# A decoder layer with a product-key expert stage on one core: the gate spread is stretched over more expert blocks, and six blocks' activations stay on chip

## The chip, the cores and the metric

One core of one Trainium2 chip runs the whole layer in one launch. The time is that of the device, in microseconds, for one execution; lower is better. The engines of the core are TensorE (PE, with its weight loads as PEld), VectorE (DVE), ScalarE (ACT), GpSimd (POOL) and SyncE (SP, which here only issues DMAs). Sixteen DMA engines serve all queues.

## What is computed

One layer over 1024 tokens of width 1024, all in float32: attention and a convolution group, a first layer norm, then the expert stage ("PEER"), a gated embedding and a second layer norm. The change touches the expert stage and the first load of the last one.

```python
def peer(x, w_query, sub_keys, u_table, v_table):          # tables: 16384 experts x 1024
    q = (xt @ w_query).reshape(t, 8, 2, 128)
    sc = einsum('thpc,hpnc->thpn', q, sub_keys)
    top_s, top_i = top_k(sc, 16)                            # per head and half
    best_s, best_c = top_k(top_s[:, :, 0, :, None] + top_s[:, :, 1, None, :], 16)
    ids = i1 * 128 + i2                                     # 128 experts per token
    gates = softmax(best_s)
    h = einsum('cd,ced->ce', x, u_table[ids])
    act = gelu(h) * gates
    return einsum('ce,ced->cd', act, v_table[ids])
...
r = ALPHA * x + peer(x, ...)
e = sigmoid(r @ w_gate) * (p @ w_ple)
x = LN2(r + e)
```

## The kernel before

The 1024 tokens are 8 tiles of 128. Tiles 0 to 2 (group A) and tiles 3 to 7 (group B, 640 tokens, `ND`) go through the expert stage in two different ways that run at the same time.

**Group A: rows.** `s_gather` fetches, for each of the 128 experts of a token, one row of U and one row of V. One step fetches 128 rows, one for each token of a tile, with an indirect DMA on GpSimd's queue (line 769, 512 KB), and VectorE uses it `ROWLAG` = 3 steps later: a product with `x1` summed into `hb` (line 777), or a multiply-add into `ag` (line 785). There are 3 x 256 = 768 such rows, with `UB` = 7 buffers. `behind` puts a row's use behind the fourth last entry of a list of marks, on VectorE's queue.

**Group B: dense.** All 16384 experts are computed for the 640 tokens, in 128 blocks of 128 experts:

- *U* (`s_early`, `u_half`): a block of U is loaded (512 KB), turned by 8 TensorE transposes, split into a high and a low part (`uu`), and multiplied with x in three products (lines 158 to 160, `mm3`), 48 matmuls of 320 columns. The low part is made by VectorE (line 665), or by TensorE with one more matmul of 512 columns for each half block and a ScalarE copy (lines 672, 674, `by_pe`). Then ScalarE takes the gelu (line 699), and the block's activations go to memory in `e_dr` (320 KB, line 700).
- *Choice* (`s_choose`): VectorE finds the experts and gates of each token of group B.
- *Spread* (`s_gates`): the gates of a token are spread over all 16384 experts as a product of two one-hot matrices. For four tokens at a time VectorE makes two comparisons (line 740) and two products (line 743) of 512 bf16 elements a partition, ScalarE makes four more products (line 745), TensorE 12 matmuls of 128 columns (line 750), ScalarE copies the sums into `stage` (line 752). Each 32 tokens the stage (2 MB) is stored in `g_dr` (line 754). A run has 160 such steps.
- *V* (`s_dense`): in sets of `SET` = 3 blocks, `v_block` loads a block of V (512 KB) and splits it (`vh`, `vl`), loads the activations from `e_dr`, multiplies them by the gates (line 878, from `gt`, six blocks a load), and splits them (`ah`, `al`), all in rings of `RING` = 7. `products` then multiplies: for each of 10 outputs, 9 matmuls of 512 columns a set. Seven outputs have a PSUM bank for the whole run (`sum`); three share one bank (`part`) and are added to `acc` by VectorE after each set (line 899).

**Order.** A program-order interleave, `weave`, puts the streams together; on it a scheduler orders each engine's queue at build time, and the queue then runs in that order. After the front part (`ORDER`) the stages are: queries of group B beside `UQ` = 9 U blocks and `RQ` = 105 rows; the choice beside `UC` = 14 blocks and `RC` = 5 rows; the spread beside 40 blocks and `RG` = 160 rows; the remaining blocks beside `RU` = 180 rows; the V stage beside the other 318 rows. The gathering pool, `VA` (U and V loads, activation buffers, `GEB` = 3) and `GT` (gates) lie on the left of SBUF; x of group B and the pages, and later the V pool, on the right.

**Final stage.** `turned` transposes and splits `r`, `gated` multiplies with the gate and embedding weights, loaded in four chunks of 256 columns by `weights` (lines 932 to 936). Its pool `Z` lies where the gathering pool was.

Of the kernel before, what the change touches and what calls it, by code (L numbers as in the profile page):

```python
# [19 lines left out]
P = 128  # L20
# [32 lines left out]
RQ, RC, RG, RU = 105, 5, 160, 180  # L53
TIE = 4
RX = 2
ZC = 3
# [20 lines left out]
def run(gen):  # L77
    for _ in gen:
        pass
# [17 lines left out]
def layer(tc, io):  # L97
# [578 lines left out]
    def s_early():  # L676

        aH, aL = act[1]
        halves = [(c, h) for c in range(P) for h in range(2)]
        ready = []  # L680
        for n in range(AHEAD):
            ready.append(u_half(*halves[n]))
            u_rest()
        for n, (c, h) in enumerate(halves):
            u_rest()
            if n + AHEAD < len(halves):
                ready.append(u_half(*halves[n + AHEAD]))
            uu = ready.pop(0)
            if h == 0:
                pss = [ph()[:, :cn] for _, cn in spl]  # L690
            for k in range(4):
                kk = 4 * h + k
                for o, (c0, cn) in zip(pss, spl):
                    mm3(o, uu[:, 0, k, :], uu[:, 1, k, :], aH[:, kk, c0:c0 + cn], aL[:, kk, c0:c0 + cn],
                              kk == 0, kk == KD - 1)
            if h:
                ge = page([P, ND], F32, "ge") if c < UA + UQ + UC else VA.tile([P, ND], F32, name="ge", bufs=GEB)
                for o, (c0, cn) in zip(pss, spl):
                    nc.scalar.activation(ge[:, c0:c0 + cn], o, AF.Gelu)
                nc.sync.dma_start(e_dr[c], ge)  # L700
                yield


    def s_gates(S_):

        iota4 = S_.tile([P, 4, P], BF, name="iota4")
        nc.vector.tensor_copy(iota4, iota_b[:, None, :].to_broadcast([P, 4, P]))

        def pairs(a):
            return a.rearrange("p e (n d) -> p e n d", d=2)  # L710
# [1 line left out]
        for j, i in enumerate(GB):  # L712
# [16 lines left out]
            nc.vector.tensor_tensor(rest, rest, sT[:, 3, :, 0], op=OP.subtract)  # L729
            for tb in range(P // TB):  # L730
                stage = S_.tile([P, P, TB], F32, name="stage", bufs=2)
                for q in range(TB // 4):
                    t = tb * TB + 4 * q

                    def col(k):
                        return sT[:, k, t:t + 4, None, :].to_broadcast([P, 4, P // 2, 2])

                    oo = S_.tile([P, 2, 4, P], BF, name="oo", bufs=2)
                    for k in range(2):
                        nc.vector.tensor_tensor(pairs(oo[:, k]), pairs(iota4), col(k), op=OP.is_equal)  # L740
                    o2 = S_.tile([P, 3, 4, P], BF, name="o2", bufs=OB)
# [6 lines left out]
                    for e in range(4):  # L748
# [4 lines left out]
                    if q == TB // 4 - 1:  # L753
# [80 lines left out]
    close(WP_p)  # L834
    VA_p, VA = pool("dense_a", "left")
    S_p, S_ = pool("spread", "left")
    weave((s_gates(S_), ND // 4), (early, SPILL - UF - UA - UQ - UC), (rows, RG))
    close(S_p)


# [5 lines left out]

    def gates(c):

        m = min(GG * SET, P - c)
        gts[c] = GT.tile([P, NB, GG * SET, TB], F32, name="gt", bufs=2)  # L850
        nc.sync.dma_start(gts[c][:, :, :m, :], g_dr[:, :, c * TB:(c + m) * TB].rearrange("b i (a t) -> i b a t", t=TB))

    left = P * 2 * NA - RQ - RC - RG - sum(int(v[2:]) for w in ORDER.split("|") for v in w.split() if v[0] == "r")
    weave((early, P - SPILL + UF), (rows, RU))
    left -= RU
# [10 lines left out]
    A_hi, A_lo, V_hi, V_lo = {}, {}, {}, {}  # L866

    def v_block(c, gt, k):
# [6 lines left out]
        ge = VA.tile([P, ND], F32, name="ge", bufs=GEB)  # L875
        nc.sync.dma_start(ge, e_dr[c])
        v = ge.rearrange("p (b t) -> p b t", t=TB)
        nc.vector.tensor_tensor(v, v, gt[:, :, k, :], op=OP.mult)  # L878
        A_hi[c] = V.tile([P, ND], F32R, name="ah", bufs=RING)
        A_lo[c] = V.tile([P, ND], F32R, name="al", bufs=RING)  # L880
        split(A_hi[c], A_lo[c], ge, nc.vector)

    def prepare(cs):
        if cs[0] % (GG * SET) == 0 and cs[0] + GG * SET < P:
            gates(cs[0] + GG * SET)
        for c in cs:
            v_block(c, gts[c - c % (GG * SET)], c % (GG * SET))
            yield

    def products(cs, o):  # L890

        j, h = o
        i, sl, hs = GB[j], slice(j * P, (j + 1) * P), slice(512 * h, 512 * h + 512)
        ps = sums[o] if o in sums else PO.tile([P, 512], F32, name="part", bufs=1)
        for c in cs:
            mm3(ps, A_hi[c][:, sl], A_lo[c][:, sl], V_hi[c][:, hs], V_lo[c][:, hs],
                c == (0 if o in sums else cs[0]), c == (P - 1 if o in sums else cs[-1]))
        if o not in sums or cs[-1] == P - 1:
            marks.append(nc.vector.tensor_tensor(acc[i][:, hs], acc[i][:, hs], ps, op=OP.add))

    def s_dense():

        sets = [list(range(c, min(c + SET, P))) for c in range(0, P, SET)]
        gates(0)
        run(prepare(sets[0]))
        for n, cs in enumerate(sets):
            ahead = prepare(sets[n + 1]) if n + 1 < len(sets) else iter(())
# [5 lines left out]
            run(ahead)  # L913

    dense = s_dense()
    n = len(outs) * -(-P // SET)
    weave((dense, n - RX), (rows, left))
    weave((dense, RX))
    run(rows)
    run(dense)  # L920
    close(V_p)
# [1 line left out]
    PP_p, PP = banks("psum_last")  # L923


    cn = 256
    wg, rT, r, bs = {}, {}, {}, {}
    ZR_p, ZR = pool("final_r", "right")

    def weights(c, pool_, eng):  # L930
        cs = slice(c * cn, (c + 1) * cn)
        raw = ZR.tile([P, KD + 2, cn], F32, name="wraw", bufs=1)
        nc.sync.dma_start(raw[:, :KD, :], io["ple_gate"][0][:, cs].rearrange("(k p) n -> p k n", p=P))
        nc.sync.dma_start(raw[:, KD:, :], io["ple_proj"][0][:, cs].rearrange("(k p) n -> p k n", p=P))
        wg[c] = [pool_.tile([P, KD + 2, cn], F32R, name=f"w{x}{c}") for x in "hl"]
        split(*wg[c], raw, eng)

    weights(0, ZR, nc.vector)
    lg, lb = bcast(io["ln2_g"][0], "ln2_g", ZR), bcast(io["ln2_b"][0], "ln2_b", ZR)
    close(GT_p)  # L940
    close(VA_p)
    close(G_p)
# [80 lines left out]
```

## Time and profile before

| | |
|---|---|
| time, median of 3 runs (lowest to highest) | 2925.62 us (2921.28 to 2936.11) |
| the profiled execution, its own time | 2930.05 us |
| its span, first to last instruction | 2928.2 us |
| mean granted TensorE clock | 0.975 of 2.4 GHz |
| TensorE, VectorE, ScalarE, GpSimd busy | 95%, 83%, 41%, 37% |
| moved by DMA | 778.11 MB, 266 GB/s over the span |

The profile is one execution. A matmul's duration in it includes a pipelined tail, so that durations of neighbours overlap; the pace is read from how many start in a stretch. A share of the DMA is the mean busy share of the 16 engines. In a row, "<-" after an idle time names what ended the wait.

### The profile page before, as it was taken

Reading aid. Unit: us, or ns where it says so; the run is one execution under the profiler, and the core shown is the slowest. Engines: PE = TensorE matmul, PEld = TensorE weight load, DVE = VectorE, ACT = ScalarE, POOL = GpSimd, SP = SyncE. Lnnn points to the kernel's source line nnn. Section 1 sums busy time; section 2 is a strip of 40 time slices with the busy share of each in tenths; the row PEclk is TensorE's granted clock in tenths of the full one; section 3 lists DMA queues with packets and bytes.
Section 4 is the critical chain, followed back from the end, with each engine's and each line's share of the span. In section 5 each row is a group of like instructions: output and inputs, shape, how many; then the busy total and the mean of one; then the engine's idle time right before and its main releaser. Section 6 shows DMA issues by size and latency. Waiting matters only on the chain.

```text
span 2928.2 us, 47594 instructions
## 1 busy us (share of the span) xinstructions
PE 2794.5 (95%) x17615; PEld 2513.3 (86%) x17615; DVE 2437.2 (83%) x5461; ACT 1193.6 (41%) x2464; POOL 1078.1 (37%) x851
## 2 busy tenths in 40 slices
PE   8996899999999999999999999799899999999888
PEld 8974589999999999999999999687788787777688
DVE  7999768979989799999856666898899888778866
ACT  4454634433334788888622222222222222222143
POOL 0103010267600333443435555555454445444320
PEclk9996899999999999999999999999999999999999
DMA  5211343599913699999999999999999999989631
GB/s 158 76 51 40 99 127 103 183 369 321 349 60 113 239 352 344 334 346 338 364 352 328 338 337 343 364 357 358 352 356 360 358 371 348 323 309 316 215 125 53
DMA packets 324569, 778.11 MB, mean 266 GB/s; under 512 B 29137, under 2 KB 144337, under 8 KB 321776
## 3 DMA queue, kind: packets, MB, share of 16 engines
q0 software_dynamic: 110592, 402.70, 38.0%
q1 hardware_dynamic: 213744, 372.37, 36.5%
q8 instruction: 138, 2.26, 0.3%
q14 instruction: 95, 0.78, 0.1%
HBM read 683.75 MB, written 91.23 MB: 265 GB/s over the span
## 4 chain that ended last, share of the span: by engine, by line
PE 79%; DVE 11%; DMA 5%; issue 3%; ACT 2%; SPq 0%; POOL 0%; DVEq 0%; ACTq 0%; POOLq 0%
PE ph L158 15%; PE ph L159 14%; PE ph L160 14%; PE sum L159 6%; PE sum L158 5%; PE sum L160 5%; PE pv L750 4%; PE pt L659 3%; PE part L158 2%; PE part L159 2%; PE part L160 2%; DMA ge<-e_dr 2%; DVE ag L785 2%; DVE row L777 1%; DVE vl L150 1%
## 5 line engine op out<-in xcount | busy, mean ns | idle before, releaser
L769 POOL DMA_INDIRECT row<-in_peer_u_dram,ids x384 | 511.5, 1332 | 707.9 <-DVE ag L785 418.7
L769 POOL DMA_INDIRECT row<-in_peer_v_dram,ids x384 | 499.5, 1301 | 647.0 <-DVE row L777 480.0
L158 PE MATMUL ph<-acth,uu 128*128 128x320 f32 x2048 | 657.4, 321 | 0.1
L159 PE MATMUL ph<-actl,uu 128*128 128x320 f32 x2048 | 641.6, 313 | 0.0
L160 PE MATMUL ph<-acth,uu 128*128 128x320 f32 x2048 | 639.9, 313 | 0.0
L785 DVE SCALAR_TENSOR_TENSOR ag<-row,hb,ag 128x1024 f32<-128x1024 f32 x384 | 492.4, 1282 | 2.2 <-DMA row<-in_peer_v_dram,ids 1.3
L777 DVE SCALAR_TENSOR_TENSOR row<-row,x 128x1024 f32<-128x1024 f32 x384 | 467.9, 1222 | 5.5 <-DMA row<-in_peer_u_dram,ids 5.2
L158 PEld LDWEIGHTS ph<-acth,uu 128*128 128x128 f32 x2048 | 386.6, 189 | 1.4 <-ACT sg L558 0.4
L159 PEld LDWEIGHTS ph<-actl,uu 128*128 128x128 f32 x2048 | 386.9, 189 | 0.7
L160 PEld LDWEIGHTS ph<-acth,uu 128*128 128x128 f32 x2048 | 385.5, 189 | 0.4
L159 PE MATMUL sum<-vl,ah 128*128 128x512 f32 x896 | 353.7, 395 | 5.0 <-DVE vl L150 4.8
L158 PE MATMUL sum<-vh,ah 128*128 128x512 f32 x896 | 344.2, 397 | 4.2 <-ACT ah L154 2.8
L154 ACT CAST ah<-ge 128x640 fp32r<-128x640 f32 x128 | 93.3, 729 | 570.7 <-DVE ge L878 417.4
L160 PE MATMUL sum<-vh,al 128*128 128x512 f32 x896 | 267.4, 390 | 0.0
L661 ACT CAST uu<-pt 128x512 fp32r<-128x512 f32 x256 | 150.5, 590 | 190.8 <-PE pt L659 181.0
L745 ACT ACTIVATE o<-oo,rest 128x128 bf16<-128x128 bf16 x640 | 205.8, 399 | 21.4 <-DVE oo L740 16.6
L158 PEld LDWEIGHTS sum<-vh,ah 128*128 128x128 f32 x896 | 171.0, 191 | 45.4 <-ACT ah L154 5.4
L159 PEld LDWEIGHTS sum<-vl,ah 128*128 128x128 f32 x896 | 171.3, 191 | 43.2 <-DVE vl L150 7.1
L158 PE MATMUL part<-vh,ah 128*128 128x512 f32 x384 | 154.7, 403 | 47.2 <-ACT ah L154 30.1
L160 PEld LDWEIGHTS sum<-vh,al 128*128 128x128 f32 x896 | 168.5, 188 | 34.9
L150 DVE TENSOR_TENSOR vl<-raw,vh 128x1024 fp32r<-128x1024 f32 x128 | 154.7, 1220 | 40.8 <-ACT vh L154 40.4
L150 DVE TENSOR_TENSOR uu<-pt,uu 128x512 fp32r<-128x512 f32 x116 | 79.8, 689 | 127.7 <-ACT uu L661 118.9
(298 smaller groups left out, 5768.3 us busy)
## 6 DMA issues: line engine op xcount, KB each, us to landing
raw<-in_peer_v_dram SPq DMA_DIRECT2D x128, 512.0 KB
raw<-in_peer_u_dram SPq DMA_DIRECT2D x89, 512.0 KB
e_dr<-ge SPq DMA_DIRECT2D x128, 320.0 KB
g_dr<-stage SPq DMA_DIRECT2D x20, 2048.0 KB
ge<-e_dr SPq DMA_DIRECT2D x128, 320.0 KB
gt<-g_dr SPq DMA_DIRECT2D x21, 1920.0 KB
uraw<-in_peer_u_dram SPq DMA_DIRECT2D x39, 512.0 KB
wraw<-in_peer_query_dram SPq DMA_DIRECT2D x32, 512.0 KB
```

The source lines that it names most:

```text
L150: return eng.tensor_tensor(o, a, b, op=OP.subtract)
L154: nc.scalar.copy(hi, src)
L158: nc.tensor.matmul(ps, lh, rh, start=first, stop=False)
L159: nc.tensor.matmul(ps, lh, rl, start=False, stop=False)
L160: nc.tensor.matmul(ps, ll, rh, start=False, stop=last)
L659: nc.tensor.matmul(ps[:, k * P:(k + 1) * P], raws[c][:, (4 * h + k) * P:(4 * h + k + 1) * P], ident, is_transpose=True, start=k == 0, stop ...
L661: nc.scalar.copy(uu[:, 0], turned)
L745: nc.scalar.mul(o2[:, 2, e], oo[:, 1, e], rest[:, t + e:t + e + 1])
L750: nc.tensor.matmul(ps[:, e * P:(e + 1) * P], o2[:, m, e], oo[:, 0, e], start=m == 0, stop=m == 2)
L769: nc.gpsimd.indirect_dma_start(out=t, out_offset=None, in_=table, in_offset=bass.IndirectOffsetOnAxis(ap=ids[i][:, s:s + 1], axis=0))
L777: behind(nc.vector.scalar_tensor_tensor(u, u, 1.0, x1, op0=OP.mult, op1=OP.mult, accum_out=hb[:, e:e + 1]), marks, TIE)
L785: behind(nc.vector.scalar_tensor_tensor(ag, v, blocks[b][:, e:e + 1], ag, op0=OP.mult, op1=OP.add), marks, TIE)
```

## The change

- The spread runs beside U until block 118 (`SPILL` 80 to 118) and takes eight tokens an instruction: 80 steps with instructions of 1024 elements and two PSUM tiles each; `o2` has 2 buffers instead of 3. TensorE still makes the low parts only for blocks below 80 (`ULOW`); the point from which one half in four goes to VectorE moves from block 39 to 47, since it hangs on `UC`.
- `UC` 14 to 22, `RC` 5 to 45 (choice), `RG` 160 to 295 (spread, beside 70 blocks), `RU` 180 to 48 (the last 13 blocks). 275 rows remain for the V stage.
- The activations of the last `KEEP` = 6 blocks are gated and split where they are made (`gated_split`), in a pool of their own, and are neither stored nor loaded. The V stage starts with these six. The ring of `ah` and `al` is that pool, six buffers.
- The first chunk of the final weights is loaded into a buffer of `gt`, issued behind the last dense step and ahead of the last rows.

```diff
-SPILL = 80
+SPILL = 118
+ULOW = 80
+KEEP = 6
-PAGES, WPAGES, RAWS, GEB, OB = 5, 6, 3, 3, 3
+PAGES, WPAGES, RAWS, GEB, OB = 5, 6, 3, 3, 2
-UA, UQ, UC, UF = 14, 9, 14, 3
-RQ, RC, RG, RU = 105, 5, 160, 180
+UA, UQ, UC, UF = 14, 9, 22, 3
+RQ, RC, RG, RU = 105, 45, 295, 48
...
-        by_pe = c < SPILL and not (2 * c > edge and c % 2 == h == 0)
+        by_pe = c < ULOW and not (2 * c > edge and c % 2 == h == 0)
...
-                nc.sync.dma_start(e_dr[c], ge)
+                if c < P - KEEP:
+                    nc.sync.dma_start(e_dr[c], ge)
+                else:
+                    gated_split(c, ge)
...
-                for q in range(TB // 4):
-                    t = tb * TB + 4 * q
+                for q in range(TB // 8):
+                    t = tb * TB + 8 * q
...
-                    ps = pv()
-                    for e in range(4):
-                        for m in range(3):
-                            nc.tensor.matmul(ps[:, e * P:(e + 1) * P], o2[:, m, e], oo[:, 0, e],
-                                             start=m == 0, stop=m == 2)
-                    nc.scalar.copy(stage[:, :, 4 * q:4 * q + 4], ps.rearrange("p (t n) -> p n t", t=4))
+                    for f4 in range(2):
+                        ps = pv()
+                        for e in range(4):
+                            for m in range(3):
+                                nc.tensor.matmul(ps[:, e * P:(e + 1) * P], o2[:, m, 4 * f4 + e], oo[:, 0, 4 * f4 + e],
+                                                 start=m == 0, stop=m == 2)
+                        nc.scalar.copy(stage[:, :, 8 * q + 4 * f4:8 * q + 4 * f4 + 4], ps.rearrange("p (t n) -> p n t", t=4))
...
+    AC_p, AC = pool("dense_acts", "left")
+    group = GG * SET
+    starts = [P - KEEP, *range(0, P - KEEP, group)]
+    first, final = P - KEEP, P - KEEP - 1
+
+    def gated_split(c, ge):
+        k = (c - first) if c >= first else c
+        gt = gts[c - k % group]
+        v = ge.rearrange("p (b t) -> p b t", t=TB)
+        nc.vector.tensor_tensor(v, v, gt[:, :, k % group, :], op=OP.mult)
+        A_hi[c] = AC.tile([P, ND], F32R, name="ah", bufs=KEEP)
+        A_lo[c] = AC.tile([P, ND], F32R, name="al", bufs=KEEP)
+        split(A_hi[c], A_lo[c], ge, nc.vector)
+
+    gates(first)
...
+        if c < first:
+            ge = VA.tile([P, ND], F32, name="ge", bufs=GEB)
+            nc.sync.dma_start(ge, e_dr[c])
+            gated_split(c, ge)
...
+    sets = [list(range(c, min(c + SET, n))) for b, n in ((first, P), (0, first)) for c in range(b, n, SET)]
...
+    raw0 = GT.tile([P, NB, group, TB], F32, name="gt", bufs=2).rearrange("p b a t -> p (b a t)")
+    raw0 = raw0[:, :(KD + 2) * cn].rearrange("p (k n) -> p k n", n=cn)
+    last_weights(0, raw0)
     run(rows)
     run(dense)
```

## Rows read from the trace of the kernel before

**Rows 1.** The page, part 1: busy us, share of the span, instructions.

```profile
PE 2794.5 (95%) x17615; PEld 2513.3 (86%) x17615; DVE 2437.2 (83%) x5461; ACT 1193.6 (41%) x2464; POOL 1078.1 (37%) x851
```

**Rows 2.** Windows: length; busy us (count) of PE, PEld, DVE, ACT, POOL; PE clock, DMA share, GB/s.

```profile
1000.00:1400.00 400.00, 400.00 (x3664) 372.45 (x3664) 368.34 (x771) 327.37 (x874) 162.22 (x135) 1.00 0.93 342
...
1500.00:1800.00 300.00, 300.00 (x2123) 299.30 (x2122) 204.85 (x278) 79.46 (x159) 156.71 (x129) 1.00 0.95 333
1840.00:1910.00 70.00, 64.60 (x271) 51.89 (x272) 61.25 (x78) 16.40 (x20) 35.64 (x28) 0.97 0.98 358
1910.00:2270.00 360.00, 349.29 (x1515) 285.28 (x1514) 320.33 (x406) 88.66 (x107) 180.54 (x132) 0.99 0.99 358
2270.00:2550.00 280.00, 268.00 (x1159) 218.24 (x1158) 242.78 (x309) 67.88 (x82) 141.00 (x99) 0.99 0.98 354
2550.00:2600.00 50.00, 50.00 (x220) 41.35 (x219) 39.73 (x51) 11.53 (x14) 20.72 (x14) 0.99 0.85 296
2600.00:2750.00 150.00, 142.26 (x607) 114.01 (x606) 119.11 (x148) 29.64 (x38) 69.36 (x48) 0.99 0.86 301
```

**Rows 3.** Timeline at the turn from U to V: start, us, engine, what.

```profile
1825.52 2.94 ACT L154 CAST vh<-raw 128x1024 fp32r<-128x1024 f32 x3
...
1826.07 0.38 SPq L876 DMA_DIRECT2D ge<-e_dr  x1
...
1838.26 0.82 DVE L878 TENSOR_TENSOR ge<-ge,gt 128x640 f32<-128x640 f32 x1
...
1839.88 0.79 PE L158 MATMUL part<-vh,ah 128*128 128x512 f32 x1 [15.18 <-ACT ah L154]
```

**Rows 4.** Timeline at the start of the final stage.

```profile
2784.20 2.33 ACT L154 CAST wh<-wraw 128x2560 fp32r<-128x2560 f32 x1 [31.73 <-DMA wraw<-in_ple_proj_dram]
...
2789.86 1.07 ACT L154 CAST rTh<-pt 128x512 fp32r<-128x512 f32 x2 [3.34 <-DMA r_dr<-ag]
...
2790.50 0.58 PE L158 MATMUL ph<-wh,rTh 128*128 128x256 f32 x1 [10.57 <-ACT rTh L154]
```

**Rows 5.** Waits, TensorE, 1840 to 2750: us in total, times, longest.

```profile
PE part L158 <- ACT ah L154: 30.1, 8, 15.2
PE part L158 <- DVE acc L899: 11.9, 10, 2.0
```

**Rows 6.** DMA queues, 1840 to 2750: packets, MB, share of 16 engines.

```profile
q0 software_dynamic: 46265, 168.46, 50.6%
q1 hardware_dynamic: 87392, 144.04, 44.7%
```

**Rows 7.** Timeline of VectorE at the end of the choice.

```profile
963.81 0.23 DVE L714 CAST f<-i1b 128x128 f32<-128x128 bf16 x1 [10.16 <-PE pt L718]
```

**Rows 8.** Windows of line 750 alone: PE busy (count), PEld, clock, DMA.

```profile
1000.00:1400.00 400.00, 139.37 (x1620) 98.79 (x1619) 1.00 0.93 342
```

**Rows 9.** DMA queues, 1000 to 1400.

```profile
q0 software_dynamic: 19529, 71.14, 50.1%
q1 hardware_dynamic: 12837, 64.85, 42.8%
```

**Rows 10.** DMA queues, 1500 to 1800.

```profile
q0 software_dynamic: 18263, 66.51, 62.9%
q1 hardware_dynamic: 11201, 33.14, 31.7%
```

**Rows 11.** Lines of VectorE by form, 1000 to 1400: busy us, mean ns, idle before.

```profile
L740 DVE TENSOR_TENSOR oo<-iota,sT 128x512 bf16<-128x512 bf16 x270 | 102.9, 424 | 26.2 <-PE pv L750 19.8 <-ACT o L745 2.3 <-issue 1.9
...
L785 DVE SCALAR_TENSOR_TENSOR ag<-row,hb,ag 128x1024 f32<-128x1024 f32 x77 | 98.5, 1280 | 0.2
L777 DVE SCALAR_TENSOR_TENSOR row<-row,x 128x1024 f32<-128x1024 f32 x58 | 70.7, 1218 | 0.0
L150 DVE TENSOR_TENSOR uu<-pt,uu 128x512 fp32r<-128x512 f32 x18 | 12.3, 685 | 0.8 <-ACT uu L661 0.8
```

**Rows 12.** Lines by form, whole run: a bf16 instruction of 1024 elements.

```profile
L575 DVE TENSOR_TENSOR u<-ge 128x1024 bf16<-128x1024 bf16 x16 | 11.6, 722 | 0.1
```

More of the change, by code (lines that the diff above doesn't have):

```diff
@@ L699, in s_early @@
                     nc.scalar.activation(ge[:, c0:c0 + cn], o, AF.Gelu)
-                nc.sync.dma_start(e_dr[c], ge)
+                if c < P - KEEP:
+                    nc.sync.dma_start(e_dr[c], ge)
+                else:
+                    gated_split(c, ge)
                 yield
     def s_gates(S_):
-        iota4 = S_.tile([P, 4, P], BF, name="iota4")
-        nc.vector.tensor_copy(iota4, iota_b[:, None, :].to_broadcast([P, 4, P]))
+        iota8 = S_.tile([P, 8, P], BF, name="iota8")
+        nc.vector.tensor_copy(iota8, iota_b[:, None, :].to_broadcast([P, 8, P]))
         def pairs(a):
@@ L731, in s_gates @@
                 stage = S_.tile([P, P, TB], F32, name="stage", bufs=2)
-                for q in range(TB // 4):
-                    t = tb * TB + 4 * q
+                for q in range(TB // 8):
+                    t = tb * TB + 8 * q
                     def col(k):
-                        return sT[:, k, t:t + 4, None, :].to_broadcast([P, 4, P // 2, 2])
-                    oo = S_.tile([P, 2, 4, P], BF, name="oo", bufs=2)
+                        return sT[:, k, t:t + 8, None, :].to_broadcast([P, 8, P // 2, 2])
+                    oo = S_.tile([P, 2, 8, P], BF, name="oo", bufs=2)
@@ L739, in s_gates @@
                     for k in range(2):
-                        nc.vector.tensor_tensor(pairs(oo[:, k]), pairs(iota4), col(k), op=OP.is_equal)
-                    o2 = S_.tile([P, 3, 4, P], BF, name="o2", bufs=OB)
+                        nc.vector.tensor_tensor(pairs(oo[:, k]), pairs(iota8), col(k), op=OP.is_equal)
+                    o2 = S_.tile([P, 3, 8, P], BF, name="o2", bufs=OB)
                     for m in range(2):
                         mark = nc.vector.tensor_tensor(pairs(o2[:, m]), pairs(oo[:, 1]), col(2 + m), op=OP.mult)
-                    for e in range(4):
+                    for e in range(8):
@@ L836, in layer @@
     S_p, S_ = pool("spread", "left")
-    weave((s_gates(S_), ND // 4), (early, SPILL - UF - UA - UQ - UC), (rows, RG))
+    weave((s_gates(S_), ND // 8), (early, SPILL - UF - UA - UQ - UC), (rows, RG))
     close(S_p)
@@ L847, in gates @@
     def gates(c):
-        m = min(GG * SET, P - c)
+        m = min(group, (P if c >= first else first) - c)
         gts[c] = GT.tile([P, NB, GG * SET, TB], F32, name="gt", bufs=2)
         nc.sync.dma_start(gts[c][:, :, :m, :], g_dr[:, :, c * TB:(c + m) * TB].rearrange("b i (a t) -> i b a t", t=TB))
+    AC_p, AC = pool("dense_acts", "left")
+    A_hi, A_lo, V_hi, V_lo = {}, {}, {}, {}
+    group = GG * SET
[10 more added lines that the diff above has]
+    gates(first)
     left = P * 2 * NA - RQ - RC - RG - sum(int(v[2:]) for w in ORDER.split("|") for v in w.split() if v[0] == "r")
@@ L874, in v_block @@
         split(V_hi[c], V_lo[c], raw, nc.vector)
[L875 to L881, printed above, removed]
+        if c < first:
+            ge = VA.tile([P, ND], F32, name="ge", bufs=GEB)
+            nc.sync.dma_start(ge, e_dr[c])
+            gated_split(c, ge)
     def prepare(cs):
-        if cs[0] % (GG * SET) == 0 and cs[0] + GG * SET < P:
-            gates(cs[0] + GG * SET)
+        if cs[0] in starts and starts.index(cs[0]) + 1 < len(starts):
+            gates(starts[starts.index(cs[0]) + 1])
         for c in cs:
-            v_block(c, gts[c - c % (GG * SET)], c % (GG * SET))
+            v_block(c)
             yield
@@ L896, in products @@
             mm3(ps, A_hi[c][:, sl], A_lo[c][:, sl], V_hi[c][:, hs], V_lo[c][:, hs],
-                c == (0 if o in sums else cs[0]), c == (P - 1 if o in sums else cs[-1]))
-        if o not in sums or cs[-1] == P - 1:
+                c == (first if o in sums else cs[0]), c == (final if o in sums else cs[-1]))
+        if o not in sums or cs[-1] == final:
             marks.append(nc.vector.tensor_tensor(acc[i][:, hs], acc[i][:, hs], ps, op=OP.add))
+    sets = [list(range(c, min(c + SET, n))) for b, n in ((first, P), (0, first)) for c in range(b, n, SET)]
     def s_dense():
-        sets = [list(range(c, min(c + SET, P))) for c in range(0, P, SET)]
-        gates(0)
         run(prepare(sets[0]))
@@ L915, in layer, with last_weights @@
     dense = s_dense()
-    n = len(outs) * -(-P // SET)
+    n = len(outs) * len(sets)
     weave((dense, n - RX), (rows, left))
+    cn = 256
+    def last_weights(c, raw):
+        cs = slice(c * cn, (c + 1) * cn)
+        nc.sync.dma_start(raw[:, :KD, :], io["ple_gate"][0][:, cs].rearrange("(k p) n -> p k n", p=P))
+        nc.sync.dma_start(raw[:, KD:, :], io["ple_proj"][0][:, cs].rearrange("(k p) n -> p k n", p=P))
     weave((dense, RX))
+    raw0 = GT.tile([P, NB, group, TB], F32, name="gt", bufs=2).rearrange("p b a t -> p (b a t)")
+    raw0 = raw0[:, :(KD + 2) * cn].rearrange("p (k n) -> p k n", n=cn)
+    last_weights(0, raw0)
     run(rows)
@@ L930, in weights @@
     def weights(c, pool_, eng):
[L931 to L934, printed above, removed]
+        if c:
+            raw = ZR.tile([P, KD + 2, cn], F32, name="wraw", bufs=1)
+            last_weights(c, raw)
         wg[c] = [pool_.tile([P, KD + 2, cn], F32R, name=f"w{x}{c}") for x in "hl"]
-        split(*wg[c], raw, eng)
+        split(*wg[c], raw if c else raw0, eng)
     weights(0, ZR, nc.vector)
     lg, lb = bcast(io["ln2_g"][0], "ln2_g", ZR), bcast(io["ln2_b"][0], "ln2_b", ZR)
+    close(AC_p)
     close(GT_p)
```

7 lines of the change are left out of this document (2 added, 5 removed).

## The prediction

> **What bounds the kernel now.** I read the page first: TensorE is busy 95% of the span [rows 1]. So the question is where TensorE is kept from running at its pace, and the windows by stage answer it [rows 2]. In the spread stage (1000 to 1400 us) it is busy all 400 us, and no wait of TensorE is listed there; in the plain U stage (1500 to 1800 us) likewise. There 2123 matmuls start in 300 us, 0.141 us each, so a block of 56 costs 7.91 us. The V stage is different: its counts fall below the 220 that the undisturbed window from 2550 us fits into 50 us (0.227 us each). From 1840 to 2750 us it starts 271 + 1515 + 1159 + 220 + 607 = 3772 matmuls, worth 857 us at that pace, in 910 us: 53 us lost. Ahead of that stands the wait of 15.18 us at the turn from U to V [rows 3], and behind the last sum another of 10.57 us [rows 4]. The change touches all of these, so it can gain; what it loads in return is the spread stage, whose room has to be worked out.
>
> Next I asked why the V stage loses. Its waits name the activation casts and the adds that free the one `part` bank [rows 5]. Behind them stand two nearly full servants. DMA: the rows' queue takes 50.6% and the other queue 44.7% of 910 us [rows 6], 460 + 407 = 867 us of transfer against TensorE's 857. VectorE: 61 + 320 + 243 + 40 + 119 = 783 us busy [rows 2]. A stage whose transfers need longer than its matmuls must lose.
>
> **The change part by part.**
>
> *U blocks.* Blocks 39 to 46 lose the VectorE finish of one half in two blocks, 4 more matmuls of 512 columns: 4 x 0.23 = +1 us. The rest of the U work is the same.
>
> *Choice.* 40 more rows come in, and 8 more U blocks. The choice had ended on VectorE and it then waited 10.16 us for TensorE's transposes [rows 7], so TensorE is the later one. It gets 8 x (7.91 + 2 x 0.23) = 67 us more, VectorE 40 x 1.25 = 50 us (a row's cost is below). Cover remains: 0, at worst 0 to +10 if rows land late and hold up VectorE's queue with the choice behind them.
>
> *Spread, TensorE.* The stage has 70 U blocks instead of 40 and as many spread matmuls. In 400 us there were 1620 of the latter [rows 8] and 2044 others [rows 2], that is 35.5 blocks of 57.5 (three halves of four finish on TensorE), 293 us; the 1620 took the remaining 107, 0.066 us each. New stage: 70 x 7.91 + 35 x 1.5 x 0.227 + 1920 x 0.066 = 554 + 12 + 127 = 693 us.
>
> *Spread, DMA.* A row cost 50.1% x 400 / 135 = 1.48 us of all 16 engines [rows 2, 9]. In the U stage the other queue's 31.7% x 300 us served 37.9 blocks, 2.5 us each [rows 10]. What remains of 42.8% x 400 in the spread, 171 - 35 x 2.5 = 84 us, served the stores of the spread, one for 96 of its matmuls, so 17 at 4.9 us [rows 8, 9]. New stage: 295 x 1.48 + 70 x 2.5 + 20 x 4.9 = 437 + 175 + 98 = 710 us. That is more than TensorE's 693. The longest stretches with full transfer show a share of 0.98 to 0.99 [rows 2]; at 0.985 the 710 us take 721, 28 more than TensorE. Row buffers (7, four ahead of use, 4 x 1.48 us) and the U blocks loaded ahead (two, 2 x 1.5) absorb some 10 of it, so I take +15. Bounds: 0, if a share of 1.02 can be had, and +48 at 0.96, which is the whole V stage's.
>
> *Spread, VectorE.* Four tokens cost two comparisons, 102.9 / 135 = 0.76 us, and as much for two products: 1.52; a row costs (98.5 + 70.7) / 135 = 1.25 [rows 11]. An instruction of 1024 elements is not in this stage; the nearest one, the bf16 add of the choice, takes 0.72 us against 0.42 for 512 [rows 11, 12]. Eight tokens so cost 4 x 0.65 to 0.72 = 2.6 to 2.9 instead of 3.04. Up to block 80 a U block brings 1.14 such steps, 4.2 rows and half a VectorE finish of 0.69 [rows 11]: 3.1 + 5.3 + 0.3 = 8.7 of 10.1 us. From 80 on it brings two finishes: 3.1 + 5.3 + 1.4 = 9.8, against TensorE's 7.91 + 27.4 x 0.066 = 9.72 us. So the last 35 blocks are full on VectorE as on DMA. It is now busy 368 of 400 us without costing TensorE [rows 2]; held to that 0.92, 35 blocks would take 35 x (9.8 / 0.92 - 9.72) = 33 us more. These are the same microseconds as the DMA's, so the +15 stands for both. Fewer marks (one for eight tokens) let rows sit deeper in VectorE's queue, and two buffers of `o2` replace three; a step now has 8.7 us, its chain some 7, so 0.
>
> *Turn from U to V.* Now the load of block 0's activations is issued at 1826.07, behind the store of block 127's; VectorE multiplies at 1838.26, ScalarE casts, and TensorE starts at 1839.88 [rows 3]. In the new order blocks 122 to 127 are gated on chip, the first sets need only `vh`, cast from 1825.52 on at about 1 us each [rows 3]: TensorE can start near 1826.6. Late next is `vl`, 1.1 us behind. Gain 13; 0 if the gates' load were late, but it can be issued when the spread ends, some 100 us before. The six gatings (VectorE 2 x 0.82, ScalarE 0.73) fall into blocks with VectorE at 205 of 300 us [rows 2]: hidden; without that cover 10 us.
>
> *V stage.* 43 rows fewer and six activation loads fewer. A row costs the DMA 460 / 320 = 1.44 us here, an activation load of 0.328 MB 407 x 0.328 / 144 = 0.9 [rows 2, 6]. DMA: 867 - 43 x 1.44 - 6 x 0.9 = 800 us; VectorE: 783 - 43 x 1.25 - 6 x 1.64 = 719; both against 857. That is 0.93 and 0.84 of TensorE's time. The old spread stage ran at DMA 0.93 and VectorE 0.92 with nothing lost. I leave 15 of the 53 us, for waits on the one `part` bank and the six `ah` (seven before: they come free a set, not a block, ahead). Gain 38; bounds 0 (the waits are of order, not of load) and 53.
>
> *End.* The first final weights move into a gates buffer, ahead of the last rows on SP's queue; their buffer has been free for a set, so nothing waits behind them. But the final stage's start hangs on the last three row sums and the store of `ag`, which frees the cast at 2789.86, and the weights had been there for their cast at 2784.20 [rows 4]. 0 there; -1 for the second chunk's earlier load, at most -4.
>
> Sum: +1 + 15 - 13 - 38 - 1 = -36, from the profiled execution's own 2930.05 to 2894. That execution ran 4.4 us above the median; I say 2892.
>
> **A rule weighed.** In the spread the 295 rows (0.524 MB each), 70 blocks (0.852) and 20 stores (2.1) are 256 MB; in 693 us that is 369 GB/s. The rows show 358 GB/s over 360 us of V stage and 342 in the spread at a share of 0.93, which is 368 at 1.0 [rows 2]. The Trainium skill, "DMA: Bandwidth & Descriptors", section "Specifications", gives an HBM limit per core of about 358 GB/s; by it, as an estimate, the stage would take 716 us, +23 before buffers. The Trainium skill under the same title, section "Bandwidth", measured 425 GB/s for a core alone; by that, nothing is lost. No long stretch here shows 425.
>
> **The rivals.**
>
> *Transfers have room.* If the share goes to 1.02 and more, the spread gives nothing back: 2894 - 15 = 2879. For: the stores leave in bursts, and a share is a mean. Against: no stretch of 280 us or more is above 0.99. The Trainium skill's 425 GB/s (the same title, section "Bandwidth") would lead here too. Chance 0.17.
>
> *The V stage's waits are of order.* VectorE's and SP's queues are in a fixed order; a cast waits because three rows stand ahead of it, whatever the load. Then only 10 to 15 of the 53 us come back: 2917 to 2922. For: whole stretches run without loss at the same load (the window from 2550). Against: that window is also the one with a share of 0.85. Chance 0.15.
>
> *Slower: the spread stage becomes the DMA's.* If the 16 engines can't be held above the 0.93 which this stage shows now, 710 us take 763, +70 instead of +15: 2894 + 55 = 2949. It decides between a share of 0.95, where 748 us eat the whole gain, and 0.93. For: 0.93 is what this mix of stores, rows and loads showed. Against: there TensorE set the pace and the transfers had idle time. Chance 0.12.
>
> **How the numbers follow.** The likeliest case, spread given back in part and V relieved, has 0.56 and its own range 2870 to 2910; then 0.17, 0.15 and 0.12. No change is a bound of these, not a case. The range for 8 in 10 goes from 2861 (spread free, V wholly relieved, end -4: 2930 + 1 - 13 - 53 - 4) to 2925, which takes in the second rival and most of the way to a spread at a share of 0.96 (2894 + 33); some 0.15 lies above it and 0.03 below. A measurement here tells about 0.5%, 15 us, from no change: below 2911 is faster, above 2940 slower. Faster: nearly all of the first two cases and a little of the third, 0.73; same 0.16; slower 0.11.
>
> **What would show it.** Right: first V matmul within 4 us of the last U matmul; blocks 45 to 114 at 10.0 to 10.4 us mean with a DMA share of 0.97 or more; V's 3840 matmuls in under 905 us; the turn to the final stage unchanged. Wrong: waits of TensorE on `o`, `uu` or U's `raw` in the spread summing to over 30 us; V windows still at 205 to 210 matmuls in 50 us; eight-token instructions near 0.84 us.

## The result and the profile after

| | before | after |
|---|---|---|
| time, median (lowest to highest, runs) | 2930.86 us (2921.28 to 2937.76, 4) | 2894.47 us (2893.70 to 2902.55, 4) |
| span of the profiled execution | 2928.2 us | 2891.9 us |

The ratio is 0.9884, its 95% interval 0.9847 to 0.9922: 34 us faster, by more than the 0.5% that can be told from no change. The profiled execution took 2893.7 us where 2894 was forecast for it. That the total came out as its sum said is luck: the spread is 32 us better than forecast, the V stage 30 and the choice 10 us worse, and these errors cancel, with 3.7 us each at the start and in the final stage. The span shows that when it is cut at points that both traces have: the first product of a U block, found by counting U's products in the timeline, and the changes of stage.

| stretch | before, us | after, us | difference | forecast |
|---|---|---|---|---|
| start to block 0 | 507.6 | 503.9 | -3.7 | 0 |
| block 0 to block 38 (queries, choice) | 462.1 | 471.6 | +9.5 | 0 |
| block 38 to last U matmul (spread, U) | 854.7 | 838.8 | -15.9 | +16 |
| last U to first V matmul | 15.5 | 1.8 | -13.7 | -13 |
| V stage, first to last matmul | 938.6 | 930.8 | -7.8 | -38 |
| to the final stage's first product | 12.0 | 11.0 | -1.0 | -1 |
| final stage | 137.7 | 134.1 | -3.7 | 0 |

The code ahead of block 0 is the same in both kernels; over all runs below it took 502 to 509 us, so the first row is spread of runs.

The page of the kernel after, part 1, answers to [rows 1]: TensorE's busy time has hardly moved, the span has.

```profile
PE 2788.4 (96%) x17619; PEld 2511.6 (87%) x17619; DVE 2397.7 (83%) x5137; ACT 1195.6 (41%) x2468; POOL 1071.4 (37%) x851
```

The windows by stage answer to [rows 2], in the same columns: choice, its tail, spread, and the V stage from 1820 us.

```profile
750.00:900.00 150.00, 141.82 (x943) 137.39 (x943) 149.18 (x575) 48.36 (x105) 94.66 (x68) 0.94 0.88 315
900.00:1050.00 150.00, 150.00 (x1054) 147.45 (x1053) 106.17 (x668) 71.84 (x141) 5.77 (x5) 1.00 0.31 106
1050.00:1700.00 650.00, 650.00 (x5666) 637.70 (x5665) 532.12 (x783) 428.93 (x1109) 299.47 (x241) 1.00 0.93 348
1820.00:1910.00 90.00, 89.22 (x381) 71.28 (x380) 75.09 (x95) 18.33 (x22) 43.74 (x33) 1.00 0.96 352
1910.00:2270.00 360.00, 351.90 (x1493) 279.88 (x1492) 305.75 (x384) 87.59 (x106) 158.38 (x122) 1.00 0.96 342
2270.00:2550.00 280.00, 271.76 (x1140) 215.70 (x1139) 245.86 (x312) 66.14 (x80) 133.44 (x100) 0.99 0.97 352
```

Three things stand in them. In the spread TensorE is busy for all 650 us at a DMA share of 0.93, where the forecast wanted 0.97 or more: TensorE is not held up, and the transfers are no fuller than before. From 900 to 1050 us the transfers idle, at a share of 0.31, and GpSimd issues next to no rows. And in the V stage TensorE is busier than before in the same stretch (351.90 of 360 us against 349.29), yet starts fewer matmuls, 1493 against 1515. Its busy time hides a slower pace.

VectorE's lines from 1050 to 1700 us answer to [rows 11]. An instruction of eight tokens takes 0.69 us, inside the forecast's 0.65 to 0.72, and VectorE's idle time ahead of it ended mostly with TensorE's spread matmuls.

```profile
L745 DVE TENSOR_TENSOR oo<-iota,sT 128x1024 bf16<-128x1024 bf16 x154 | 99.2, 688 | 73.4 <-PE pv L756 56.8 <-PE pt L661 10.7 <-ACT uu L663 2.3
```

For rows that had still to land VectorE waited 4.3 us in these 650.

```profile
DVE row L783 <- DMA row<-in_peer_u_dram,ids: 3.5, 3, 2.0
DVE ag L791 <- DMA row<-in_peer_v_dram,ids: 0.8, 1, 0.8
```

The timeline at the turn answers to [rows 3]: 1.77 us from the last U matmul's start to the first of V, and only casts of `vh` are waited for.

```profile
1814.29 0.31 PE L162 MATMUL ph<-acth,uu 128*128 128x320 f32 x1
1816.06 0.50 PE L160 MATMUL part<-vh,ah 128*128 128x512 f32 x1 [1.46 <-ACT vh L156]
```

The waits of TensorE from 1820 to 2740 us answer to [rows 5], with the wait at the turn outside them in this case.

```profile
PE part L160 <- DVE acc L918: 11.5, 14, 1.2
PE part L160 <- ACT ah L156: 6.5, 3, 4.2
```

The DMA queues from 1816 to 2747 us answer to [rows 6]. The rows' queue moves as much as before, 168.14 MB against 168.46.

```profile
q0 software_dynamic: 46182, 168.14, 49.2%
q1 hardware_dynamic: 88980, 146.56, 45.0%
```

So does the count of row issues on GpSimd in the V stage (lines, busy, mean ns, idle before): 169 + 150 = 319, against 326 in the kernel before. The diff emits 275 rows there. The rows were put there at build time: in VectorE's queue 443 uses of a row stand ahead of the first `vl`, of 493 emitted ahead of the V stage (before: 430 of 450), and the same 443 in e1, e5, e8 and e10.

```profile
L775 POOL DMA_INDIRECT row<-in_peer_v_dram,ids x169 | 225.2, 1333 | 255.2 <-DVE row L783 181.3 <-DVE ag L791 41.8 <-issue 24.0
L775 POOL DMA_INDIRECT row<-in_peer_u_dram,ids x150 | 197.9, 1319 | 235.3 <-DVE ag L791 185.7 <-issue 25.1 <-DVE row L783 23.2
```

The slower pace shows in the timeline of the V stage: eleven starts from 2000.03 to 2002.38, 0.235 us apart, at a granted clock of 1.00 of 2.4 GHz.

```profile
2000.03 0.40 PE L161 MATMUL sum<-vl,ah 128*128 128x512 f32 x1
2000.27 0.40 PE L162 MATMUL sum<-vh,al 128*128 128x512 f32 x1
...
2002.15 0.39 PE L162 MATMUL part<-vh,al 128*128 128x512 f32 x1
2002.38 0.40 PE L160 MATMUL part<-vh,ah 128*128 128x512 f32 x1
```

Averaged over all undelayed neighbours in the stage it is 234.3 ns, and 234.2 to 234.3 in every stretch of 50 us; before it was 227.1. For 3840 matmuls that is 28 us. "Stalls" below are what a V stage takes beyond its own pace times its 3840 matmuls.

The start of the final stage answers to [rows 4]: its wait is as long as before, though the first weights now come from a `gt` buffer and are cast at once.

```profile
2746.95 2.33 ACT L156 CAST wh<-gt 128x2560 fp32r<-128x2560 f32 x1 [20.03 <-PE part L162]
...
2757.21 1.07 ACT L156 CAST rTh<-pt 128x512 fp32r<-128x512 f32 x2 [7.94 <-DMA r_dr<-ag]
...
2757.85 0.58 PE L160 MATMUL ph<-wh,rTh 128*128 128x256 f32 x1 [10.11 <-ACT rTh L156]
```

### The profile page after: what moved, and what is told of

It reads as the page before. It is cut to its first block, busy times and chain, and to the rows that moved or that the text cites. A ratio compares the mean times of both kernels' runs of the same rounds, so it can differ in the third digit from the quotient of the medians.

```text
span 2891.9 us, 47040 instructions
## 1 busy us (share of the span) xinstructions
PE 2788.4 (96%) x17619; PEld 2511.6 (87%) x17619; DVE 2397.7 (83%) x5137; ACT 1195.6 (41%) x2468; POOL 1071.4 (37%) x851
## 4 chain that ended last, share of the span: by engine, by line
PE 87%; DVE 9%; issue 1%; DMA 1%; ACT 1%; SPq 0%; POOL 0%; ACTq 0%; DVEq 0%
PE ph L160 15%; PE ph L161 15%; PE ph L162 15%; PE sum L160 7%; PE sum L161 7%; PE sum L162 6%; PE pv L756 4%; PE pt L661 4%; PE part L160 3%; PE part L162 3%; PE part L161 3%; DVE ag L791 1%; PE pt L674 1%; DVE cv L357 1%; DVE row L783 1%
## 5 line engine op out<-in xcount | busy, mean ns | idle before, releaser
L775 POOL DMA_INDIRECT row<-in_peer_v_dram,ids x384 | 513.1, 1336 | 705.6 <-DVE row L783 538.0
L775 POOL DMA_INDIRECT row<-in_peer_u_dram,ids x384 | 491.7, 1281 | 620.9 <-DVE ag L791 312.4
L160 PE MATMUL sum<-vh,ah 128*128 128x512 f32 x896 | 337.0, 399 | 1.3 <-ACT vh L156 0.9
L162 PE MATMUL sum<-vh,al 128*128 128x512 f32 x896 | 291.9, 396 | 0.0
L750 ACT ACTIVATE o<-oo,rest 128x128 bf16<-128x128 bf16 x640 | 196.7, 392 | 30.6 <-DVE oo L745 25.9
L701 ACT ACTIVATE ge<-ph 128x320 f32<-128x320 f32 x256 | 108.7, 437 | 217.7 <-PE ph L162 183.7
L160 PE MATMUL part<-vh,ah 128*128 128x512 f32 x384 | 155.0, 404 | 21.8 <-DVE acc L918 13.7
```

Of the source, the lines that this page charges most:

```text
L160: nc.tensor.matmul(ps, lh, rh, start=first, stop=False)
L162: nc.tensor.matmul(ps, ll, rh, start=False, stop=last)
L775: nc.gpsimd.indirect_dma_start(out=t, out_offset=None, in_=table, in_offset=bass.IndirectOffsetOnAxis(ap=ids[i][:, s:s + 1], axis=0))
```

## The experiments

Theory at the outset: the slower matmuls come from where `ah` and `al` lie now, and the rows which the diff took out of the V stage never left it. One execution each; the last run, with five more, stands below the table. Block 38 and the first V matmul are counted from the start of the span, so these columns carry the 502 to 509 us that a run took to block 0.

| run | time, us | block 38 | first V matmul | V stage, us | pace, ns | stalls, us | rows issued in V |
|---|---|---|---|---|---|---|---|
| before | 2930.05 | 969.7 | 1839.9 | 938.6 | 227.1 | 67 | 326 |
| after | 2893.70 | 975.5 | 1816.1 | 930.8 | 234.3 | 31 | 319 |
| e1, 32 bytes | 2891.10 | 978.4 | 1819.0 | 925.7 | 232.6 | 33 | 319 |
| e2, before with `vh` moved | 2943.74 | 968.8 | 1839.0 | 952.9 | 233.4 | 57 | 326 |
| e3, four tokens | 2921.75 | 982.1 | 1827.1 | 948.1 | 234.2 | 49 | 319 |
| e4, 40 rows to V | 2937.38 | 966.9 | 1807.5 | 965.0 | 234.2 | 66 | 348 |
| e5, 416 bytes | 2872.57 | 978.1 | 1818.7 | 908.0 | 226.9 | 37 | 319 |
| e6, rows after choice | 2894.56 | 960.8 | 1803.2 | 945.0 | 234.2 | 46 | 326 |
| e7, old order of blocks | 2929.55 | 981.1 | 1832.5 | 950.3 | 234.2 | 51 | 316 |
| e8, e5 less 46 rows | 2858.83 | 978.4 | 1819.0 | 896.2 | 226.8 | 25 | 273 |
| e10, e5, all moved | 2878.62 | 984.3 | 1824.7 | 907.7 | 227.0 | 36 | 319 |
| e11, e5, 40 rows more early | 2872.16 | 978.3 | 1820.3 | 906.0 | 226.9 | 35 | 295 |
| e12, e5 with e6's rows | 2884.60 | 966.1 | 1808.5 | 929.0 | 227.1 | 57 | 326 |

### Where the operands lie: e1, e2, e5, e10

```diff
     AC_p, AC = pool("dense_acts", "left")
+    nc.vector.memset(AC.tile([P, 8], F32, name="pad"), 0.0)      # e1; 104 in place of 8 in e5, 96 in e10
...
         split(V_hi[c], V_lo[c], raw, nc.vector)
+        if c == 0:                                               # e2, in the kernel before; e10 likewise, so that vh and vl move too
+            nc.vector.memset(V.tile([P, 8], F32, name="pad"), 0.0)
```

> The changed kernel with a 32-byte tile ahead of the six ah and al tiles, so that these start 32 bytes past a multiple of 64 as vh and vl do. In the changed kernel a V matmul of 512 columns takes 234.3 ns against 227.0 before, everywhere in the stage. Theory: it is the offset of the stationary tile against the moving one; then the pace is 227 ns again, 3840 x 7.3 ns = 28 us less of matmul work, of which DMA and VectorE let through 15 to 28: 2866 to 2880 us. Rival: it is the region of SBUF, the ring of six or the order of the blocks; then the pace stays at 234 and the time within 5 us of 2894.

> The kernel before with a 32-byte tile between the vl and the ah tiles, which moves vh and vl to a multiple of 64 while ah and al stay 32 bytes past one. Theory of the offset between the two: the pace goes from 227 to 234 ns; as the stage has some 53 us of stalls, which take up part of it, the time rises by 5 to 28 us over 2930. A theory that only the stationary tile's own offset counts, and the theory of region, ring or order, both give 227 ns and no change within 8 us.

> The changed kernel with 416 bytes ahead of the ah and al tiles in place of the 32 of the first run. In the kernel before, ah and vh lie a multiple of 512 bytes apart (57344), in the changed kernel 37792, in the run with 32 bytes 37760, neither a multiple of 512; with 416 bytes it is 37376 = 73 x 512. Theory of the distance: 227 ns a matmul again, 28 us less of matmul work. How much of it the V stage shows tells what sets its end: 20 to 28 us (2866 to 2875) if it is TensorE, under 10 us (2884 to 2894) if transfers or VectorE are. Rival, region or ring: 232 to 234 ns and 2890 to 2894 us.

> The run with 416 bytes, with ah, al, vh and vl all placed 32 bytes lower: the distance of 37376 = 73 x 512 bytes stays, the addresses are now multiples of 64 and leave 448 in place of 480 when divided by 512. Theory of the distance: 227 ns a matmul, 2870 to 2876 us. Rival, the residue of the addresses themselves (480 in the kernel before and in the run with 416 bytes): 232 to 235 ns and 2890 to 2897 us.

The first two gave half an answer: moving `vh` by 32 bytes in the old kernel costs 6.3 ns a matmul (e2's time is 13.7 us above the table's execution of the kernel before and 7 above one timed beside it, 2936.57 us, both inside the 5 to 28 expected), so the place does count, but giving `ah` the same offset from a multiple of 64 in the new one brought 1.7 ns and no more. With the distance of the two tiles made 73 x 512 bytes, e5 runs at 226.9 ns, and e10, with all four kinds of tile 32 bytes lower and the same distance, at 227.0. By distance from the first `vh` to the first `ah`, as the build assigns them: 57344 and 37376 (112 and 73 times 512) 226.9 to 227.1; 57376, 37760 and 37792 232.6 to 234.3. e10's time of 2878.62 us lies above the 2870 to 2876 that were expected, but not for its V stage, which took 907.7 us against e5's 908.0: its block 0 started 4 us later. The same stretch of e5's timeline, with 0.226 us from start to start:

```profile
1999.85 0.39 PE L160 MATMUL part<-vh,ah 128*128 128x512 f32 x1
...
2001.44 0.39 PE L161 MATMUL sum<-vl,ah 128*128 128x512 f32 x1
2001.66 0.39 PE L162 MATMUL sum<-vh,al 128*128 128x512 f32 x1
```

The V stage became 22.8 us shorter in e5. Of 28 us of slower matmuls the stalls had hidden 5 (they are 31 us in the kernel after and 37 in e5), so it is TensorE, not the transfers, that sets most of this stage.

### Rows in the V stage: e4, e8, e11

e4 sets `RC` from 45 to 5. e8 deletes the last 46 row steps, so that part of the last token tile isn't computed. e11 emits 45 rows beside the choice's first fourteen blocks and 40 behind its end.

```diff
-RQ, RC, RG, RU = 105, 45, 295, 48
+RQ, RC, RG, RU = 105, 5, 295, 48                                # e4
...
+            if i == GA[-1]:                                      # e8, on e5; `left` is 46 less too
+                del order[-46:]
...
-    weave((s_choose(1), 8 * nB), (early, UC), (rows, RC))
+    weave((s_choose(1), 8 * nB), (early, 14), (rows, 45))        # e11, on e5; 5 in e6 and e12
+    marks.extend(chosen[-1:] * TIE)                              # the choice's last instruction on VectorE
+    weave((early, 8), (rows, 40))                                # 60 in e6 and e12
```

> The changed kernel with 5 rows beside the choice in place of 45; the 40 run in the V stage. Theory of the choice: the 40 rows hold up VectorE's queue with the choice behind them, and blocks 0 to 38 take 9.5 us longer for it; without them block 38 starts 8 to 10 us sooner. Rival: the eight further U blocks there cost it; then it stays within 3 us. V stage: 40 rows are 58 us of transfer and 50 of VectorE. Theory of load: the stage, with 34 us of stalls against its own pace, loses 15 to 30 us more. Theory of order: its stalls stay within 6 us.

> The run with 416 bytes, and the last 46 of the 768 row steps left out (part of the last token tile's output is not computed), so that the V stage runs the 275 rows that the prediction gave it and not 321. Theory of load: its 28 us of stalls against its own pace fall to 15 or less, and the stage gains 15 to 45 us on the same kernel with all rows. Theory of order: VectorE's and SP's order stays, and the gain is under 8 us.

> The run with 416 bytes, with 85 rows beside the choice: 45 with its first fourteen U blocks, as in the changed kernel, and 40 held behind its last instruction, where transfers idle from 950 to 1045 us. VectorE's order then has 467 rows ahead of the first vl in place of 443. Theory of load: the V stage loses 24 rows, at 12 us for 46 that is 6 us, and the rows after the choice cost nothing: 2862 to 2868. Rival: VectorE has no room for them between choice and spread: block 80 starts 8 to 15 us later than in the run with 416 bytes, and the time is 2872 to 2882.

e4 confirms the choice's part: block 38 starts 8.6 us sooner without the 40 rows, and 10.6 when counted from block 0. VectorE's windows (800 to 900 us, then 900 to 1000) show where they had been; first the kernel after, with 45 GpSimd instructions in the first one:

```profile
800.00:900.00 100.00, 94.65 (x640) 92.01 (x639) 99.83 (x422) 30.67 (x68) 61.70 (x45) 0.95 0.84 299
900.00:1000.00 100.00, 100.00 (x695) 98.36 (x694) 91.89 (x643) 48.84 (x87) 0.00 (x0) 1.00 0.35 119
```

and e4, where the choice's instructions take their place and VectorE is half idle a window later:

```profile
800.00:900.00 100.00, 100.00 (x706) 98.76 (x705) 98.57 (x684) 42.22 (x84) 10.24 (x7) 1.00 0.34 112
900.00:1000.00 100.00, 100.00 (x695) 98.26 (x693) 49.68 (x329) 40.95 (x78) 0.00 (x0) 1.00 0.35 119
```

In its V stage 29 more rows are issued and 35 us more are stalled, above the 15 to 30 of the theory of load; 11 further rows run behind it, and the last row sums then hold up the final stage by 28.28 us instead of 10.11:

```profile
2802.49 0.58 PE L160 MATMUL ph<-wh,rTh 128*128 128x256 f32 x1 [28.28 <-ACT rTh L156]
```

Fewer rows give less back than more rows cost: 46 fewer, 11.8 us in e8 (between the 15 or more of load and the 8 or less of order, with 25 us of stalls left of e5's 37); 24 fewer, 2.0 us in e11, whose time is that of e5 although VectorE had room for the rows (block 80 starts 1.6 us later). In e4, e8 and e11 VectorE's other instructions in the V stage, too, stand in another order than in the kernel after. So none of the three changes the load and keeps the order.

### Rows behind the choice: e6, e12

> The changed kernel, where of the 45 rows emitted beside the choice 5 stay, and 60 are emitted with its last eight U blocks and held behind the choice's last instruction on VectorE. Theory: in the changed kernel the rows run from 800 to 900 us ahead of the choice on VectorE and push it back by some 9 us, and from 900 to 1045 the transfers idle at a share of 0.35. Then block 38 starts at 966 to 968 us, rows run between 950 and 1045, and the spread's end and the V stage stay as they were: 2882 to 2888. Rival: rows on VectorE push the spread's first steps back by as much; then the start of block 80 shows no gain, 2890 to 2896.

> The run with 416 bytes with the rows of the run that held 60 of them behind the choice. That run had the V stage 13 us sooner and 14 us longer. Theory: the stage's end is set by the rows and loads that are left, so an earlier start is given back, and it ends as with 416 bytes alone: 2868 to 2876. Rival: it was the slower matmuls that took it; then 2855 to 2862.

e6's time lies in the rival's range, but by neither's mechanism. The choice and the spread kept the gain: rows ran in the idle stretch (a share of 0.72 from 900 to 1000 us), block 38 came 14.7 us sooner and V 12.9 us (13.4 and 11.6 from block 0). But the V stage took 14.2 us longer.

```profile
900.00:1000.00 100.00, 100.00 (x695) 98.38 (x694) 85.56 (x322) 41.11 (x78) 40.04 (x34) 1.00 0.72 272
```

e12, at the faster pace, started V 10 us sooner than e5 and needed 21 us more, with 7 rows more in it: worse than either theory. Its waits of TensorE in the V stage are longer on both counts; first e5, then e12:

```profile
PE part L160 <- DVE acc L919: 14.2, 16, 1.3
PE part L160 <- ACT ah L156: 8.2, 4, 4.4
```

```profile
PE part L160 <- DVE acc L923: 21.2, 20, 2.4
PE part L160 <- ACT ah L156: 13.2, 6, 3.3
```

e3 shows the same with no row more: 319 rows, 49 us of stalls against 31. After, e1, e5 and e10, which have one and the same order of VectorE's queue, lie at 31 to 37. In e3, e6 and e12 the scheduler put rows, casts and adds into another order. That this order makes the stalls is argued from these counts; no run changes it alone.

### Tokens a step: e3

The spread's body of before (12 matmuls a step, 160 steps) in the kernel after:

```diff
-                for q in range(TB // 8):
-                    t = tb * TB + 8 * q
+                for q in range(TB // 4):
+                    t = tb * TB + 4 * q
```

> The changed kernel with the spread's body of before: four tokens a step, three buffers of o2. Theory: the spread runs at TensorE's pace, and the eight-token step saves switches between its short matmuls and U's; then 70 blocks go from 9.28 to 9.5 us in the stretch of blocks 80 to 115 and from 9.5 to 9.8 or more before, in all +12 to +25 us. Rival, the prediction's: transfers set the pace of this stage; then it takes the same time within 4 us. A third: VectorE is at its limit with four tokens; then waits of TensorE on ps and o2 appear and it is +25 to +50 us.

From block 38 to the end of U it took 843.5 us against 839.1: 4.4 us, not 12 to 25, and just outside the 4 of the rival. That transfers don't set the pace here shows in TensorE's waits instead: 0.2 us in the whole stretch, in both. (The run's 28 us are these, 6.6 us up to block 38, and 17 in the V stage, of which above.) So the step's size explains a small part of what the spread gained. The timeline of the kernel before points to the rest: it goes to the spread's matmuls twice a step.

```profile
1200.71 0.31 PE L160 MATMUL ph<-acth,uu 128*128 128x320 f32 x1
1200.87 0.23 PE L750 MATMUL pv<-oo,o 128*128 128x128 bf16 x1
1200.90 0.39 PE L158 MATMUL ph<-acth,uu 128*128 128x320 f32 x1
1201.13 0.31 PE L159 MATMUL ph<-actl,uu 128*128 128x320 f32 x1
1201.28 0.31 PE L160 MATMUL ph<-acth,uu 128*128 128x320 f32 x1
1201.42 0.30 PE L158 MATMUL ph<-acth,uu 128*128 128x320 f32 x1
1201.57 0.79 PE L750 MATMUL pv<-oo,o 128*128 128x128 bf16 x11
```

Three U starts follow 1200.71 in 0.57 us, where three intervals of 0.147 take 0.44: one visit for a single spread matmul cost 0.13 us. Medians from block 38 to the end of U say what of it is the visit's: a U matmul starts 147 ns after another U matmul and a spread matmul 56 ns after another, but a visit takes 151 ns from the last U start to the first spread start, 29 back to U, and 230 from that U start to the next. So a visit costs 151 + 29 + 230 - 2 x 147 - 56 = 60 ns beyond its matmuls. The kernel before makes 336 visits for its 1920 spread matmuls. The kernel after does all 24 of a step in one go,

```profile
1501.83 0.31 PE L162 MATMUL ph<-acth,uu 128*128 128x320 f32 x1
1501.97 1.51 PE L756 MATMUL pv<-oo,o 128*128 128x128 bf16 x24
```

and makes 86 visits; e3 lies in between, with 172. At 0.06 us these are 15 us between before and after, where 15.9 were measured, and 5 between e3 and after, where 4.4 were. This is worked out from counts; no run changes the visits alone.

### The order of blocks: e7

```diff
-    starts = [P - KEEP, *range(0, P - KEEP, group)]
-    first, final = P - KEEP, P - KEEP - 1
+    starts = [*range(0, P, group)]
+    first, final = 0, P - 1
```

All activations are stored and loaded again.

> The changed kernel with the V stage in the order of before, block 0 first, and all activations stored and loaded again; the gates' first load stays early, the ring of six too. Theory of the turn: the first V matmul waits for load, product and cast of block 0's activations, 12 to 15 us after the last U matmul in place of 1.5; the V stage takes six loads and gatings more, 0 to 6 us. In all +10 to +20. Rival: the wait is made up in the V stage, since its transfers run on meanwhile: then +0 to +5.

```profile
1832.52 0.80 PE L160 MATMUL part<-vh,ah 128*128 128x512 f32 x1 [12.34 <-ACT ah L156]
```

The turn costs 10.8 us more, as the theory had it. The rest of the +36 is more than it had: 19.5 us in the V stage, 4.2 ahead of block 0 and 1.4 before block 38.

### The version that beats both: e5, five rounds

> The changed kernel with 416 bytes ahead of ah and al, timed in five rounds beside the kernel before. Theory of the distance: 2868 to 2880 us, a ratio of 0.979 to 0.984 to the kernel before, 15 to 26 us under the changed kernel. If the 2872.57 of one execution was a lucky one: 2884 to 2895.

It took 2874.67 us (2870.76 to 2881.16, 5 runs) against 2929.42 (2924.24 to 2937.45, 9 runs) for the kernel before: a ratio of 0.9816, 95% interval 0.9792 to 0.984. All five lie below the kernel after's four (2893.70 to 2902.55).

## Why the prediction came out right, and where it was wrong

The total is right by luck, as the table of stretches shows; the terms one by one:

**Turn (-13).** Right, with its mechanism: -13.7, and e7 brings the wait back.

**Choice (0, at worst +10).** At the bound, +9.5: rows ahead of the choice on VectorE, as named there (e4: 10.6 us from block 0). But they didn't "land late": from 510 to 980 us VectorE waited 2.5 us for rows to land. It was full, 99.83 of the 100 us from 800. The step that failed is "TensorE is the later one": one wait at the choice's end didn't show that VectorE had room for 50 us of rows.

**Spread (+15, with TensorE at 693 us).** The wrong step is "I take +15" for the transfers: TensorE waited for none. The 710 us of transfers that this was worked out from never came together: of the 295 rows emitted beside the 70 blocks 251 were issued there, and 44 of those emitted ahead of the V stage ran in it (319 issued, 275 emitted). VectorE's queue had been ordered so at build time, and VectorE waited 4.3 us for rows to land, so the transfers of the run did not push the rows out; why the scheduler put them there stays open. So neither this estimate nor the rule weighed in the prediction was put to the test: the limit of about 358 GB/s in the Trainium skill, "DMA: Bandwidth & Descriptors", section "Specifications", was not exceeded by the 348 GB/s over 650 us. The other error was in TensorE's own term. The 0.066 us a spread matmul, taken from the kernel before, contained its visits; with 56 ns a matmul and 86 visits at 60 ns it would have been some 14 us less, and the 70 blocks did take 680 us, 13 less than 693. 15 + 14 = 29 of the 32 us by which the term missed.

**V stage (-38).** Measured -7.8, and the step that failed is "43 rows fewer": 7 fewer were issued there, since the scheduler had put rows of the spread behind it. On top came a cost that the prediction didn't have, the pace of 234.3 ns: 22.8 us, by e5. With the pace mended the stage gains 30.6 us, and with 46 rows really gone (e8) 42.4. The share of load, the cause that I gave for these stalls, stays unclear: 24 rows fewer gave back 2.0 us and 46 fewer 11.8, far below the 1.44 us a row that they were priced at as transfer, but 29 more cost 34.2 (e4), and in each of these runs the order changed too. The second rival, waits of order, has e3 on its side: the rows of after, and 18 us more stalls. Its size doesn't hold: it left 10 to 15 us to come back, and by the table's measure 30 of 67 did at the mended pace, though the rows had stayed. How much of e7's 19.5 us belongs to starting on six blocks that need no load, and how much to another order of VectorE's queue, stays open: no run here changes the blocks and keeps that order.

**The signs.** The turn of 1.8 us and the start of the final stage came as named for "right". Blocks 45 to 114 took 9.7 us each at a share of 0.91, below the 10.0 to 10.4 at 0.97 or more that were named; the V stage took 930.8 us, not under 905; and its windows of 50 us held 207 matmuls on average from 1910 to 2270, a sign named for "wrong".

**End (-1).** Right for the wait; the final stage itself gained 3.7 us. The second chunk's loads, issued at 2746.66, before the wait instead of behind it, were given up to 4 us for it. No run undoes that alone.

## What to carry to other kernels

A stretch in which an engine is "busy all the time" may still hold time to be won: count instructions per microsecond, before and after, in the same stage. When work with no early consumer is moved to a fuller stage, the scheduler may put it behind that stage's end, so look where it was issued, not where the program emits it. And a total that meets its forecast says little: compare it stage by stage. Where a pool is moved, compare the pace of one unchanged instruction on both sides.

## What was not expected of the hardware

A matmul of 512 float32 columns has its pace set by how far its two operands lie apart: 226.9 to 227.1 ns from start to start for three placements with a multiple of 512 bytes between the first stationary and the first moving tile, 232.6 to 234.3 for three others, at the full granted clock. The tiles are whole multiples of 512 bytes long, so what remains of the distance is the same for every pair of them. The Trainium skill, "TensorE: Matmul & The Clock Gate", section "Back-to-back issue gap", gives the interval as a function of the columns alone, about 216 ns for 512 for a matmul by itself and about 131 in a stream of weight loads and matmuls; no run here shows either, and the place adds 3%. Whether 512 bytes is the smallest distance that does it wasn't tried: of multiples of 64 or 128 that are not of 512, one was (37760), and it was slow.

A visit of TensorE to the spread's matmuls costs 0.06 us beyond them, by the medians above. After spread matmuls and after transposes alike, the first U matmul is followed only 0.23 us later, in place of 0.147.

The transfers reached a share of 1.01 at 394 GB/s in e11, from 1000 to 1050 us, where the longest stretches here stay at 340 to 360.

```profile
1000.00:1050.00 50.00, 48.99 (x338) 47.95 (x337) 38.57 (x56) 15.70 (x34) 34.29 (x30) 1.00 1.01 394
```
